# Two decoder layers on one core: the first block's attention weights turned by VectorE in squares of 32 that go round by DRAM, in place of TensorE transposes

## The chip, the cores and the metric

One core of one Trainium2 chip. The time is device microseconds of one execution; three runs of the kernel before are given. "Block" below means a block of 128 tokens: the sequence has 256, so there are two, 0 and 1. "Layer" means one of the two decoder layers.

## The reference

Each of the two layers takes x (256 tokens by 1024 channels, f32) through a half-step SwiGLU, a normalisation, three token mixers that run on the same stream, an output projection with another normalisation, and a second SwiGLU with a third. Two of the mixers are softmax attention, and the change touches only these:

```python
def memory_cross_attention(q, mem_n, w_mem_kv):
    k, v = jnp.split(mem_n @ w_mem_kv, 2, axis=-1)          # 256 memory rows, 4 heads of 128
    s = jnp.einsum('bshd,bmhd->bhsm', q, k).astype(jnp.float32) * (XA_DH ** -0.5)
    p = jax.nn.softmax(s, axis=-1)
    o = jnp.einsum('bhsm,bmhd->bshd', p.astype(v.dtype), v)

def sliding_window_attention(q, k, v, sinks):                # 8 query heads, 2 key heads of 64, window 128
    s = jnp.where(mask, einsum('bnqhgd,bnkhd->bnhgqk', qb, kb) * dh ** -0.5, NEG_INF)
    m = jnp.maximum(s.max(-1, keepdims=True), sink)
    p = jnp.exp(s - m)
    p = p / (p.sum(-1, keepdims=True) + jnp.exp(sink - m))
    o = jnp.einsum('bnhgqk,bnkhd->bnqhgd', p.astype(v.dtype), vb)
```

The third mixer is a gated delta rule with a triangular solve of 64 by 64 chunks. It is not touched, but shares the engines.

## The kernel before

All weights come as one stream of units, 128 by 1024 f32 (512 KB), in the order of use. `unit` loads one into a tile `raw` (four buffers) from the SP queue, and ScalarE and VectorE `split` it into a rounded part `whi` and a rest `wlo` (five buffers each, line 125). A product of two such split operands is three matmuls (`mm3`, line 134). TensorE therefore does 12 matmuls of 512 columns for one unit in most stages, and the other engines prepare the next units meanwhile.

A scheduler orders each engine's instructions; inside `mixers` TensorE's own are pinned to the order in which the program is written. Every engine runs its list in order: an instruction that waits holds up all that stand behind it on the same engine or queue. The DMAs that `nc.sync` starts stand in SP's list among the weight loads, those of `nc.gpsimd` in POOL's list among its arithmetic.

`weave(work, steps)` writes one stage of dense matmuls and puts small pieces of attention or delta rule between its steps. The stages of the mixers that matter here, in order, are `halves(xt, use_sq)` (four steps), `gates(0)` (eight), `branch(0, oX)` (four), `gates(1)` (eight).

- Memory attention: `x_scores(tb)` leaves the softmax of block tb in `prs[tb]`, 128 queries on the partitions by 4 heads by 256 memory rows. `x_turn(tb)` brings the memory rows to the partitions: 8 TensorE transposes of 128 by 128 through the identity (line 137) into PSUM, then one copy by ScalarE and one by VectorE into `pt` (line 711). `x_values(tb)` multiplies with the values (`at<-pt,u`).
- Sliding attention: `w_scores(tb, hh)` for two halves hh of the heads, `w_turn(tb, hh)` with the same kind of transposes and copies (line 766), `w_values(tb)` (`at<-pt,swv`). For block 0 there is one block of keys, so 4 transposes per half.
- The inverse of the delta rule: `inverses` makes, on POOL, masked copies `l` (line 798), sends a small tile to DRAM (`dr`, line 791), reads it back spread over the partitions (`w<-dr`, line 795) and runs 15 steps of elimination (lines 807 and 808), ending in `Y32` (line 809). `begin_inverse` then lets VectorE transpose it (line 902); the matmuls of `double` follow right after `w_values(0)`.

The SwiGLU stages already turn their own tiles by the way that the change uses: VectorE transposes each 32 by 32 square (line 356), four DMAs write the squares to a DRAM tile `tr` from POOL (line 362), and one DMA reads them back in the turned order (line 363).

## Time and profile before

| | |
|---|---|
| three runs | 1274.08 us median (1273.45 to 1274.12) |
| span of the profiled execution, first to last instruction | 1272.1 us |
| its own time from start to end | not given; the median of the runs is 2.0 us above its span |
| granted TensorE clock, mean | 0.998 |
| TensorE: busy time of the span | 1260.6 us, 99% |
| VectorE, ScalarE, POOL busy | 864.1, 661.4, 207.2 us |
| DMA | 261.40 MB, mean 205 GB/s |

The page lists busy time by engine, then the chain of work that ended last and the costliest groups. Because matmuls are pipelined, a group's "mean ns of one" is the time one instruction is in flight; what it costs in a row of its kind is read from the starts of neighbours in the timeline. A timeline row gives start, duration, engine, line, operation, output and inputs, the count of merged instructions, and in brackets the idle time before it with what ended it.

### The profile page before, as it was taken

How to read it: one execution, taken by the hardware profiler on the slowest of the kernel's cores; microseconds unless marked ns; L12 is line 12 of the kernel's file. 1: busy time of each engine (PE TensorE's matmuls, PEld its weight loads, DVE VectorE, ACT ScalarE, POOL GpSimd, SP SyncE). 2: the span in 40 equal slices, each digit the busy share in tenths (PEclk: the TensorE clock that was granted, in tenths of full speed). 3: DMA queues.
4: the chain of work that ended last, by engine and by line, in shares of the span. 5: the costliest groups of instructions: out<-in, count | busy, mean ns of one | idle time of the engine just before them, and what ended most of it. 6: DMA issues, size and time to landing. Idle time of an engine off the chain costs nothing.

```text
span 1272.1 us, 18768 instructions
## 1 busy us (share of the span) xinstructions
PE 1260.6 (99%) x6948; PEld 1073.3 (84%) x6948; DVE 864.1 (68%) x1274; ACT 661.4 (52%) x982; POOL 207.2 (16%) x365
## 2 busy tenths in 40 slices
PE   9999999999999999999999999999999999999997
PEld 6888889999778888888888888899987788888886
DVE  6678576886647776665766665759867387766565
ACT  6456444655664544454454554456556554454441
POOL 1232000002311102221012220000023101122100
PEclk9999999999999999999999999999999999999999
DMA  8988765655534748877668877566463356577762
GB/s 294 317 271 289 248 208 159 211 171 129 172 117 144 241 141 259 241 241 220 217 210 244 256 252 219 177 185 213 150 167 134 100 189 225 174 246 244 241 220 82
DMA packets 77643, 261.40 MB, mean 205 GB/s; under 512 B 11920, under 2 KB 13328, under 8 KB 77552
## 3 DMA queue, kind: packets, MB, share of 16 engines
q1 hardware_dynamic: 66320, 232.40, 56.0%
q0 software_dynamic: 11088, 27.68, 8.1%
q8 instruction: 54, 0.88, 0.3%
q14 instruction: 37, 0.30, 0.1%
q10 hardware_dynamic: 144, 0.13, 0.0%
HBM read 246.40 MB, written 13.76 MB: 205 GB/s over the span
## 4 chain that ended last, share of the span: by engine, by line
PE 89%; DMA 3%; POOL 3%; DVE 2%; issue 2%; ACT 0%; SPq 0%; DVEq 0%; POOLq 0%; ACTq 0%
PE acc L134 80%; PE at L134 3%; PE sm L134 2%; DMA w<-dr 2%; PE sm L137 2%; DVE wlo L125 1%; DMA raw<-in_wst_dram 1%; POOL t L808 1%; POOL t L807 1%; PE acc L332 1%; PE acc L333 1%; POOL l L798 1%; PE acc L335 1%; DMA dr<-t 1%; ACT whi L125 0%
## 5 line engine op out<-in xcount | busy, mean ns | idle before, releaser
L125 DVE TENSOR_TENSOR wlo<-raw,whi 128x1024 fp32r<-128x1024 f32 (+2 forms) x405 | 487.0, 1210 | 279.7 <-ACT whi L125 277.5
L125 ACT CAST whi<-raw 128x1024 fp32r<-128x1024 f32 (+2 forms) x405 | 413.7, 1029 | 400.6 <-PE acc L134 316.2
L134 PE MATMUL acc<-whi,hT 128*128 128x512 f32 (+1 forms) x1824 | 562.2, 386 | 0.5 <-ACT whi L125 0.5
L134 PEld LDWEIGHTS acc<-whi,hT 128*128 128x128 f32 x1824 | 340.0, 188 | 69.8 <-ACT whi L125 2.3
L134 PE MATMUL acc<-wlo,hT 128*128 128x512 f32 (+1 forms) x912 | 350.2, 384 | 0.0
L134 PE MATMUL acc<-whi,u 128*128 128x512 f32 x812 | 259.5, 392 | 0.0
L134 PEld LDWEIGHTS acc<-wlo,hT 128*128 128x128 f32 x912 | 171.3, 188 | 33.1 <-DVE wlo L125 1.0
L134 PEld LDWEIGHTS acc<-whi,u 128*128 128x128 f32 x812 | 152.3, 188 | 32.1 <-DVE u L125 0.5
L134 PE MATMUL acc<-wlo,u 128*128 128x512 f32 x406 | 158.2, 390 | 0.0
L362 POOL DMA_DIRECT2D tr<-t x176 | 96.3, 554 | 311.6 <-DVE t L356 303.5
L134 PE MATMUL acc<-hT,whi 128*128 128x256 f32 x672 | 122.2, 284 | 0.0
L134 PEld LDWEIGHTS acc<-hT,whi 128*128 128x128 f32 x672 | 104.6, 192 | 0.0
L134 PE MATMUL acc<-hT,wlo 128*128 128x256 f32 x336 | 95.0, 283 | 0.0
L134 PEld LDWEIGHTS acc<-wlo,u 128*128 128x128 f32 x406 | 76.3, 188 | 15.4
L134 PEld LDWEIGHTS acc<-hT,wlo 128*128 128x128 f32 x336 | 64.3, 191 | 0.0
L363 POOL DMA_DIRECT2D pt<-tr x44 | 25.0, 569 | 192.5 <-DMA tr<-t 138.4
L353 ACT ACTIVATE t<-acc 128x256 f32<-128x256 f32 x88 | 33.5, 381 | 36.9 <-PE acc L134 36.9
L134 PE MATMUL acc<-u,u 128*128 128x512 f32 x186 | 46.4, 394 | 0.0
L354 DVE TENSOR_TENSOR t<-t,acc 128x256 f32<-128x256 f32 x88 | 36.6, 417 | 8.1 <-ACT t L353 4.1
L1000 POOL TENSOR_TENSOR u<-u,gt 128x512 f32<-128x512 f32 x16 | 20.7, 1294 | 125.0 <-DVE gt L998 125.0
L134 PEld LDWEIGHTS acc<-u,u 128*128 128x128 f32 x186 | 34.6, 188 | 7.5
L125 DVE TENSOR_TENSOR u<-pt,u 128x512 fp32r<-128x512 f32 x44 | 28.9, 657 | 9.4 <-ACT u L125 9.4
(236 smaller groups left out, 1165.0 us busy)
## 6 DMA issues: line engine op xcount, KB each, us to landing
raw<-in_wst_dram SPq DMA_DIRECT2D x409, 512.0 KB, 4.4
tr<-t POOLq DMA_DIRECT2D x176, 64.0 KB, 3.8
pt<-tr POOLq DMA_DIRECT2D x44, 256.0 KB, 5.0
raw<-in_wst_dram SPq DMA_DIRECT2D x16, 324.0 KB, 3.0
gB<-in_lnp_dram SPq DMA_DIRECT2D x6, 512.0 KB, 5.8
bB<-in_lnp_dram SPq DMA_DIRECT2D x6, 512.0 KB, 6.2
w<-dr POOLq DMA_DIRECT2D x4, 512.0 KB, 12.0
t<-in_xT_dram SPq DMA_DIRECT2D x4, 256.0 KB, 5.2
```

What stands on the lines that cost most here:

```text
L125: return nc.scalar.copy(hi, src).ins, nc.vector.tensor_tensor(lo, src, hi.bitcast(F32), op=ALU.subtract).ins
L134: return pe(nc.tensor.matmul(*a, **k))
L137: return pe(nc.tensor.transpose(*a))
L332: nc.tensor.matmul(ps, hT[0][:, k, ts], hi[:, c], start=k == 0, stop=False)
L333: nc.tensor.matmul(ps, hT[0][:, k, ts], lo[:, c], start=False, stop=False)
L335: nc.tensor.matmul(ps, hT[1][:, k, ts], hi[:, c], start=False, stop=k == KD - 1)
L353: act = nc.scalar.activation(t[:, :, tb, :], g, AF.Silu).ins
L354: ins = nc.vector.tensor_tensor(t[:, :, tb, :], t[:, :, tb, :], u, op=ALU.mult).ins
L362: nc.gpsimd.dma_start(d[:, :, q].rearrange("b c x -> c b x"), z[32 * q:32 * q + 32].rearrange("c (b x) -> c b x", b=4))
L363: back = nc.gpsimd.dma_start(y, d.rearrange("b c q x -> (b c) (q x)")).ins
L798: nc.gpsimd.tensor_tensor(L32[q, c], AK[c][q, :, 0, q], cs[q, C_LV:C_LV + 32].unsqueeze(1).to_broadcast([32, 4, 32]), op=ALU.mult)
L1000: nc.gpsimd.tensor_tensor(mg[tb][:, js], mg[tb][:, js], gt[tb][:, js], op=ALU.add)
```

## The change

For block 0 the TensorE transposes and their copies go. A new `square` lets VectorE transpose the 32 by 32 squares of a 128 by 512 tile, writes the result to a DRAM tile by four DMAs and reads it back by one, 256 KB each way. Memory attention does this twice per layer in a new `x_leave` (POOL's queue, DRAM tile `tx`), called in step 3 of `halves(xt, use_sq)`; the call of `x_turn(0)` goes. Sliding attention does it once for each half inside `w_turn(0, hh)` (SP's queue, DRAM tile `tw`). The matmuls of `x_values(0)` and `w_values(0)` read the new layout, and the split behind `w_values(0)` becomes two splits of half the size. Block 1 stays as it is. In one run of the kernel all this happens twice, once per layer.

```diff
+        def square(src, order, queue, dst, tag):
+
+            z = T(p2, [P, 512], "t2", bufs=4)
+            nc.vector.transpose(z, src)
+            d = T(pd, [4, 32, 4, P], tag)
+            for a in range(4):
+                queue.dma_start(d[:, :, a].rearrange("m x c -> x m c"), z[32 * a:32 * a + 32].rearrange("x (m c) -> x m c", m=4))
+            order.append(lambda: queue.dma_start(dst, d.rearrange("m x a c -> (m x) (a c)")))
+
+        def x_leave():
+            pT = prs[2] = T(p2, [P, 2, 4, 4, 32], "pt")
+            backs = []
+            for kb in range(2):
+                square(prs[0][:, :, kb * P:(kb + 1) * P].rearrange("p h (m x) -> p m h x", m=4), backs, nc.gpsimd, pT[:, kb].rearrange("p a h x -> p (a h x)"), "tx")
+            for f in backs:
+                f()
+
...
-                    matmul(ps[:, h, :], mv_[:, kb, h * P:(h + 1) * P], prs[2 + tb][:, kb, h, :], start=kb == 0, stop=kb == 1)
+                    matmul(ps[:, h, :], mv_[:, kb, h * P:(h + 1) * P], prs[2 + tb][:, kb, h, :] if tb else prs[2][:, kb, :, h, :], start=kb == 0, stop=kb == 1)
...
         def w_turn(tb, hh):
             if hh == 0:
                 wpT[tb] = [T(p2, [P, 2, 4, P], "pt") for _ in range(tb + 1)]
+            if tb == 0:
+                backs = []
+                square(wpr[0, hh][:, :, 0:P].rearrange("p j (m x) -> p m j x", m=4), backs, nc.sync, wpT[0][0][:, hh].rearrange("p a x -> p (a x)"), "tw")
+                backs[0]()
+                return
...
-                    matmul(pso[hs, :], swv[:, kb, hs], wpT[tb][kb][:, kv].rearrange("p h q -> p (h q)"), start=kb == 0, stop=kb == tb)
-            split(oS[0][:, :, ts], oS[1][:, :, ts], pso.rearrange("p (h k) -> p h k", h=4))
+                    r = wpT[tb][kb][:, kv].rearrange("p h q -> p (h q)") if tb else wpT[0][0].rearrange("p y a (i v x) -> p (y a) i v x", i=2, v=2)[:, :, :, kv]
+                    matmul(pso[hs, :] if tb else pso[hs, :].rearrange("p (y i x) -> p y i x", y=8, i=2), swv[:, kb, hs], r, start=kb == 0, stop=kb == tb)
+            if tb:
+                split(oS[0][:, :, ts], oS[1][:, :, ts], pso.rearrange("p (h k) -> p h k", h=4))
+            else:
+                for y in range(2):
+                    split(*(t[:, 2 * y:2 * y + 2, ts].rearrange("p i (a x) -> p i a x", a=4) for t in oS), pso[:, y * S:y * S + S].rearrange("p (a i x) -> p i a x", a=4, i=2))
...
-            3: [lambda: spread(1)],
+            3: [lambda: spread(1), x_leave],
...
-            3: [lambda: x_turn(0)],
```

Where the scheduler puts the new instructions is read from the built programs. In the changed kernel's numbering, 711 is the write and 712 the read back of `square`, 708 its transpose, and the lines that follow them in `mixers` have moved by 27 (798 is 825, 902 is 929).

On POOL, from the two products that open the delta rule (line 678) to the inverse's DMA into `dr`, before:

```order
L678 TENSOR_TENSOR w_462_2591<-cs,g_2586 128x512
L798 TENSOR_TENSOR l_469_2600<-u_463_2592,cs 32x128 x4
L798 TENSOR_TENSOR l_469_2600<-u_464_2593,cs 32x128 x4
L803 COPY t_535_3053<-cs 128x128
L791 DMA dr_3041<-t_531_3034 128x128
```

The same place now (`tx` are the two DRAM tiles of memory attention, `pt` the turned weights that `x_values(0)` reads):

```order
L678 TENSOR_TENSOR w_462_2591<-cs,g_2586 128x512
L711 DMA tx_2925<-t_513_2923 32x4x128 x4
L711 DMA tx_2932<-t_515_2930 32x4x128 x4
L712 DMA pt_2922<-tx_2925 128x512
L825 TENSOR_TENSOR l_469_2600<-u_463_2592,cs 32x128 x4
L825 TENSOR_TENSOR l_469_2600<-u_464_2593,cs 32x128 x4
L712 DMA pt_2922<-tx_2932 128x512
L830 COPY t_540_3070<-cs 128x128
L818 DMA dr_3058<-t_536_3051 128x128
```

Ten DMAs stand ahead of the inverse's `dr`, and the second read back stands behind all eight masked copies `l`.

On VectorE, from the last sum of the sliding softmax of block 0 to the weight splits of `gates(1)`, before:

```order
L754 TENSOR_TENSOR sums_3308<-sums_3308,sk_3309 128x4
L755 RECIPROCAL sums_3308<-sums_3308 128x4
L902 STREAM_TRANSPOSE w_470_2601<-w_470_2601 128x256
L125 TENSOR_TENSOR wlo_3517<-raw_3515,whi_3516 128x1024
L125 TENSOR_TENSOR wlo_3564<-raw_3562,whi_3563 128x1024
```

The same place now (`pp_3302` is the softmax of the second half of the heads, `t_602` its turned squares):

```order
L771 TENSOR_TENSOR sums_3312<-sums_3312,sk_3313 128x4
L772 RECIPROCAL sums_3312<-sums_3312 128x4
L929 STREAM_TRANSPOSE w_470_2601<-w_470_2601 128x256
L708 STREAM_TRANSPOSE t_602_3406<-pp_3302 128x512
L125 TENSOR_TENSOR wlo_3527<-raw_3525,whi_3526 128x1024
L125 TENSOR_TENSOR wlo_3574<-raw_3572,whi_3573 128x1024
```

The second half's transpose stands behind line 929, which waits for POOL's inverse to end; the first half's (`t_599`) stands four rows ahead of line 929.

On SP's queue, among the weight loads of `gates(1)` and of what follows it, before:

```order
L115 DMA raw_3640<-in_wst_dram 128x1024
L115 DMA raw_3694<-in_wst_dram 128x1024
L115 DMA raw_3746<-in_wst_dram 128x1024
L115 DMA raw_3795<-in_wst_dram 128x1024
L115 DMA raw_3827<-in_wst_dram 128x1024
L115 DMA raw_3833<-in_wst_dram 128x1024
```

The same loads now (`tw` are the DRAM tiles of the two halves, `pt` the turned weights that `w_values(0)` reads; `raw_3650` is the load called `raw_3640` before):

```order
L115 DMA raw_3650<-in_wst_dram 128x1024
L711 DMA tw_3386<-t_599_3384 32x4x128 x4
L711 DMA tw_3408<-t_602_3406 32x4x128 x2
L712 DMA pt_3383<-tw_3386 128x512
L711 DMA tw_3408<-t_602_3406 32x4x128
L115 DMA raw_3704<-in_wst_dram 128x1024
L115 DMA raw_3756<-in_wst_dram 128x1024
L711 DMA tw_3408<-t_602_3406 32x4x128
L115 DMA raw_3805<-in_wst_dram 128x1024
L115 DMA raw_3837<-in_wst_dram 128x1024
L712 DMA pt_3383<-tw_3408 128x512
L115 DMA raw_3843<-in_wst_dram 128x1024
```

The second half's last write and its read back have moved in behind weight loads that wait for buffers. The second layer has the same orders in all three places.

## The prediction

> **What bounds the kernel now.** I read the page's busy times first, then its chain of work, then TensorE's waits, then the timeline of the mixers of the first layer.

> ```profile
> PE 1260.6 (99%) x6948; PEld 1073.3 (84%) x6948; DVE 864.1 (68%) x1274; ACT 661.4 (52%) x982; POOL 207.2 (16%) x365
> ...
> PE 89%; DMA 3%; POOL 3%; DVE 2%; issue 2%; ACT 0%; SPq 0%; DVEq 0%; POOLq 0%; ACTq 0%
> ```

> TensorE is busy for 99% of the span and carries 89% of the chain, so its work and its waits are the time. The view of waits shows how little it waits in the mixers; this is the only row there that concerns attention:

> ```profile
> PE at L134 <- DVE pp L741: 0.8, 2, 0.6
> ```

> Two waits, one in each layer, 0.8 us together and 0.6 the longest. The chain in order of time (start, duration, what) says what this wait hangs on:

> ```profile
> 306.68 3.32 DMA dr<-t
> ...
> 336.46 0.75 POOL w L809
> 337.61 0.51 DVE wlo L125
> ...
> 342.20 0.61 DVE pp L741
> 342.86 1.08 PE at L134 x4
> ```

> The inverse's trip through DRAM and its POOL work end at 337.2, VectorE's weight splits stood behind it, then its line 741, and `w_values(0)` starts 0.6 us late at 342.86. So at that place the inverse has no slack: what delays POOL's `dr` delays TensorE.

> **What is saved.** The group of the attention transposes, and TensorE's timeline in the first layer: a product of the delta rule, the 8 transposes of `x_turn(0)`, `x_values(0)`, the first `w_turn(0, .)`, `w_values(0)` and the inverse's matmuls.

> ```profile
> L137 PE MATMUL at<-cs,pp 128*128 128x128 f32 x80 | 10.9, 275 | 0.0
> ```

> ```profile
> 298.39 0.38 PE L134 MATMUL sm<-u 128*128 128x128 f32 x2
> ...
> 305.42 0.39 PE L134 MATMUL acc<-whi,hT 128*128 128x512 f32 x1
> 305.65 1.03 PE L137 MATMUL at<-cs,pp 128*128 128x128 f32 x8
> 306.44 0.48 PE L134 MATMUL acc<-whi,hT 128*128 128x512 f32 x1
> 306.76 0.39 PE L134 MATMUL acc<-wlo,hT 128*128 128x512 f32 x1
> ...
> 309.28 1.95 PE L134 MATMUL at<-pt,u 128*128 128x128 f32 x16
> 310.98 0.48 PE L134 MATMUL acc<-whi,hT 128*128 128x512 f32 x1
> ...
> 331.55 0.60 PE L137 MATMUL at<-cs,pp 128*128 128x128 f32 x4
> 331.90 0.47 PE L134 MATMUL acc<-whi,u 128*128 128x512 f32 x1
> 332.21 0.39 PE L134 MATMUL acc<-wlo,u 128*128 128x512 f32 x1
> ...
> 342.86 1.08 PE L134 MATMUL at<-pt,swv 128*64 128x512 f32 x4 [0.61 <-DVE pp L741]
> 343.86 1.51 PE L134 MATMUL sm<-w,l 32*32 32x32 f32 x64
> ```

> From 305.65 to 306.44 the 8 transposes take 0.79 us, and the matmul behind them starts its successor after 0.32 instead of 0.23 us: 0.88 us. Each half of `w_turn` takes 331.90 - 331.55 = 0.35, plus 0.08 in the same way: 0.44, and the two 0.88. Together 1.76 us per layer, 3.5 us in all. ScalarE loses three copies and VectorE one per layer, 0.6 to 0.7 us each beside dense matmuls: they count nothing.

> **What VectorE gets.** Four transposes per layer, which the SwiGLU's own show:

> ```profile
> L356 DVE STREAM_TRANSPOSE t<-t 128x512 f32<-128x512 f32 x44 | 31.3, 711 | 1.3
> ```

> 0.71 us each. The first two stand behind the softmax of block 0:

> ```profile
> 293.45 0.90 ACT L701 ACTIVATE pp<-pp,sums 128x256 f32<-128x256 f32 x2
> ```

> ```profile
> 293.91 1.22 DVE L125 TENSOR_TENSOR wlo<-raw,whi 128x1024 fp32r<-128x1024 f32 x1
> 295.05 1.26 DVE L675 SCALAR_TENSOR_TENSOR u<-w,cS,sm 128x256 f32<-128x256 f32 x3
> ...
> 337.24 0.45 DVE L902 STREAM_TRANSPOSE w<-w 128x256 f32<-128x256 f32 x1 [4.52 <-POOL w L809]
> 337.61 4.59 DVE L125 TENSOR_TENSOR wlo<-raw,whi 128x1024 fp32r<-128x1024 f32 x4
> ```

> The softmax ends at 293.45 + 0.90 = 294.35, VectorE's split at 295.1, so the transposes run to 295.8 and 296.5. The three products at 295.05 slip by 1.4 us, to 297.7; TensorE reuses their banks at 298.39, so nothing waits. The two halves of the split behind `w_values(0)` lie beside dense matmuls: nothing.

> **First wait: `x_values(0)`.** POOL's list has the eight writes, one read back, the masked copies `l`, the other read back, then the inverse's `dr`. POOL's timeline, with one set of four writes from a SwiGLU stage:

> ```profile
> 97.48 2.18 POOL L362 DMA_DIRECT2D tr<-t  x4 [3.55 <-DVE t L356]
> ...
> 296.39 2.51 POOL L798 TENSOR_TENSOR l<-u,cs 32x128 f32<-32x128 f32 x4 [14.84 <-DVE u L675]
> 302.96 3.42 POOL L798 TENSOR_TENSOR l<-u,cs 32x128 f32<-32x128 f32 x4 [4.06 <-DVE u L675]
> 306.44 0.29 POOL L803 COPY t<-cs 128x128 f32<-128x128 f32 x1
> 306.68 0.60 POOL L791 DMA_DIRECT2D dr<-t  x1
> ...
> 336.46 0.74 POOL L809 TENSOR_TENSOR w<-t,cs 128x256 f32<-128x256 f32 x1
> ```

> The next two rows are issue to landing of the SwiGLU's writes (64 KB) and read backs (256 KB), the same sizes as here:

> ```profile
> DMA to landing us min/median/max: 2.0/3.8/6.0
> ...
> DMA to landing us min/median/max: 3.1/5.0/6.9
> ```

> First four writes 295.8 to 298.0, the others to 300.2. The last of the first four starts at 297.5 and lands 3.8 later, 301.3. The read back takes 0.57 to issue (the SwiGLU's line 363 has the same shape): 301.9. Then both sets of `l`, 2.51 + 3.42 = 5.9 us: 307.8. Only then goes the second read back, and lands 5.0 later at 312.8. TensorE, 0.88 us earlier than before, stands at `x_values(0)` at 308.4: it waits **4.4 us**. With the shortest landings (2.0, where the eight writes end later, and 3.1) it is 1.4, with the longest (6.0, 6.9) 8.5. I take the medians: same sizes, same queue. Behind POOL's waits stand `l` and the inverse's `dr`, which the next part follows.

> **Second wait: `w_values(0)`.** `dr` goes at 307.8 + 0.57 + 0.29 (line 803) = 308.7 instead of 306.68, so the inverse ends 2.0 later, 339.2, and line 902 at 339.6. VectorE's order now has the second half's transpose behind line 902: 340.3. The four weight splits, 4.59 in all, end at 341.5, 342.6, 343.8 and 344.9. On SP's queue the half's fourth write stands behind two weight loads, which wait for the first two of these splits to free their buffers: it goes at 342.6 and lands 3.8 later, 346.4. The first half's read back, ahead of it, is long done. The second's follows, and `w_values(0)` needs both. For its landing I take SP's own loads:

> ```profile
> raw<-in_wst_dram SPq DMA_DIRECT2D x409, 512.0 KB, 4.4
> ```

> 4.4 us (they are twice as large, but the read back has two of them ahead): 350.8. TensorE is there at 342.25 (342.86 less its wait of 0.61) + 3.5 (first wait's end against 309.28) - 0.88 = 344.9: **5.9 us**, and the old waits are gone (0.8 in both layers). With 2.0 and 3.1 it is about 3, with 6.0 and 6.9 about 10.6. The loads on SP that are held up cost nothing more, as TensorE stands meanwhile and four split units lie ready; were that cover gone, each unit would be late by what the queue waits, 1 to 4 us.

> **After the waits.** The only long idle time of TensorE in this trace is at the start:

> ```profile
> 1.52 3.75 PE L1080 MATMUL sm<-pp 128*128 128x512 f32 x4 [1.52 <-DVE pp L1077]
> 5.04 0.74 PE L134 MATMUL acc<-whi,hT 128*128 128x512 f32 x2
> ```

> ```profile
> core 0: 1272.1 us, clock 0.998
> ```

> Four rows of f32 matmuls of 512 columns (the trace counts such a matmul twice) take 5.04 - 1.52 = 3.5 us, 0.88 each. In mid-run, 16 of 128 columns take 310.98 - 309.28 = 1.70, which is 0.43 for 512 columns. So TensorE starts at half its rate for some 3.9 us, and the run's mean granted clock leaves room for that: 0.002 x 1272 = 2.5 us. If it does so after 5.9 us of waiting, the four matmuls of `w_values(0)` (343.86 - 342.86) take 1.0 more, and I allow 0.3 for what follows, since the 64 small ones may be bound otherwise: 1.3 us, between 0 and 2.0. After 4.4 us I take none; the upper end is 1.7, the whole of `x_values(0)`.

> [...]

> **Sum.** Per layer 4.4 + 5.9 + 1.3 - 1.76 = 9.8 us. The second layer has the same orders, so I take twice that less the old waits, 19.7 - 0.8 = 18.9 us. The span of 1272.1 becomes 1291.0; the median of the runs lies 2.0 above the span, so 1293.0 us.

> [...]

> **The rivals.**
> - *Everything lands in time.* Then the transposes and the old waits go and nothing comes: 1274.1 - 3.5 - 0.8 = 1269.8, the other side. For it: `x_leave` is called two stages before its use. It needs the second read back issued by 308.4 - 5.0 = 303.4, where POOL still has its second set of `l` to do, and the second sliding half down by 344.9, 4.6 us after its transpose, with two landings between. Both would have to give way: 0.04.
> - *Only the sliding wait bites.* If the read back lands near the shortest 3.1 us and POOL's copies run faster without VectorE beside them, `x_values(0)` waits little: per layer 5.9 + 1.3 - 1.76 = 5.4, less 0.8 in all, the time 1284.2. The DMA engines' share of 0.40 in the window from 300 to 310 us (the column before the GB/s) speaks for it, the POOL order against: 0.17.

> ```profile
> 300.00:310.00 10.00, 10.00 (x54) 8.48 (x54) 7.85 (x14) 7.13 (x17) 4.02 (x6) 1.00 0.40 116
> ```

> - *Slow rate after both waits, and long landings.* `x_values(0)` at half rate adds 1.7 and the slow stretch of the second wait up to 0.7 more: 1293.0 + 4.8 = 1297.8; with landings 1 us over the median, two to a wait, 8 more, some 1306. The waits are the longest idle times of the run, the rows for it are the start's alone: 0.18.

> The change itself is done as described; the transposes really leave TensorE's list.

> **How the numbers follow.** My forecast, both waits at about the medians, has 0.61, between 1286 and 1300. Beyond it lie the sliding wait alone below and the long landings above, so 1282 to 1306 leaves about 2 in 10 out. A difference under 0.2% (2.5 us) could not be told from none. Faster by more than that is the first rival, 0.04; within it, one wait gone and the other at its shortest, 0.03; slower 0.93.

> **What would show it.** In the trace of the changed kernel: 32 fewer transposes in the group `at<-cs,pp` (48 of 80 left); TensorE idle before the first `at<-pt,u` of a layer and before the first `at<-pt,swv`, released by the DMAs `pt<-tx` and `pt<-tw`; `dr` issued some 2 us later against the POOL copies; SP's fourth `tw` write after two weight loads. The prediction is wrong if those two idle times are short, if weights come late behind SP's queue, or if TensorE stays slow for long after them.

## The result, and the profile after

The changed kernel takes 1304.03 us (median of 4 runs, 1300.28 to 1305.07); the kernel before, timed beside it, 1274.1 (4 runs, 1273.45 to 1274.55). The ratio is 1.0226, 95% interval 1.0214 to 1.0238: 29.9 us slower. The forecast was 1293.0, in a range from 1282 to 1306. The direction and the places were right; the size was not, and nearly all of this part is about where the other 11 us come from. The profiled execution took 1303.62 us with a span of 1301.8.

The busy times of the changed kernel:

```profile
PE 1268.5 (97%) x6916; PEld 1078.0 (83%) x6916; DVE 868.4 (67%) x1282; ACT 657.9 (51%) x978; POOL 218.9 (17%) x385
```

TensorE does 32 matmul rows less (6916 for 6948) and is nevertheless busy 7.9 us longer (1268.5 for 1260.6): some of its work went slower. The rest of the 29.7 us by which the span grew is idle time, and the view of TensorE's waits names it (total, times, longest):

```profile
PE at L134 <- DMA pt<-tw: 11.4, 1, 11.4
PE at L134 <- issue: 6.3, 1, 6.3
PE at L134 <- DMA pt<-tx: 4.9, 2, 2.7
```

`pt<-tw` is the read back of the sliding squares, `pt<-tx` that of the memory squares. The second row is the same place in the second layer, `w_values(0)`, where the view names no releaser; it is the read back too, which was issued at 995.19 and landed 3.2 us later, at 998.4, just ahead of the start at 998.51. So `w_values(0)` waits 11.4 and 6.3 us, `x_values(0)` 2.2 and 2.7. The group of attention transposes has shrunk as announced, from 80 rows to 48:

```profile
L137 PE MATMUL at<-cs,pp 128*128 128x128 f32 x48 | 6.4, 277 | 0.0
```

TensorE's timeline around the two places in the first layer, and `x_values(0)` and `w_values(0)` of the second:

```profile
309.80 0.38 PE L134 MATMUL at<-pt,u 128*128 128x128 f32 x2
312.37 1.83 PE L134 MATMUL at<-pt,u 128*128 128x128 f32 x14 [2.19 <-DMA pt<-tx]
...
343.90 0.39 PE L134 MATMUL acc<-whi,hT 128*128 128x512 f32 x1
355.72 1.97 PE L134 MATMUL at<-pt,swv 128*64 128x512 f32 x4 [11.43 <-DMA pt<-tw]
357.62 2.31 PE L134 MATMUL sm<-w,l 32*32 32x32 f32 x64
359.87 0.80 PE L134 MATMUL acc<-whi,hT 128*128 128x512 f32 x1
...
365.15 0.86 PE L134 MATMUL at<-swk,u 128*128 128x512 f32 x2
...
958.64 2.53 PE L134 MATMUL at<-pt,u 128*128 128x128 f32 x14 [2.70 <-DMA pt<-tx]
...
998.51 1.98 PE L134 MATMUL at<-pt,swv 128*64 128x512 f32 x4 [6.32 <-issue]
```

`x_values(0)` starts on the half that has come first, its first two rows, and then waits for the other. Behind the long wait everything is slow: the four rows of `w_values(0)` take 1.90 us (357.62 - 355.72; before 1.00), the 64 small ones 2.25 (before 1.44), and the dense matmuls from 359.87 to 365.15 take 5.3 (before 2.9). The windows around it say why. Columns: start and end, length, the engines' busy times, then the granted clock, the DMA share and GB/s:

```profile
348.00:349.00 1.00, 0.00 (x0) 0.00 (x0) 0.67 (x1) 0.00 (x0) 0.00 (x0) 0.80 1.03 331
349.00:365.00 16.00, 9.28 (x80) 6.57 (x81) 2.82 (x8) 6.20 (x18) 0.00 (x0) 0.50 0.33 116
365.00:366.00 1.00, 1.00 (x4) 0.76 (x4) 0.00 (x0) 0.61 (x1) 0.00 (x0) 0.67 0.00 0
```

The granted clock falls to a half some 4.3 us into the wait and comes back at 365.7, 10 us after TensorE has work again: 17 us of half clock (0.4 + 16 + 0.7), of which about 10 hit work. From 355.72 to 365.15, 9.4 us, TensorE does what took it 5.3 before (342.86 to 348.19): 4.1 us lost to the clock. The same reckoning gives 3.9 behind `w_values(0)` of the second layer (9.2 for 5.3), and about 1.7 behind its `x_values(0)`, where the clock is at a half for 3.4 us: its 14 rows take 2.53 us where those of the first layer take 1.83, and the rest falls on the dense matmuls behind them.

Why the squares come so late is on three other engines. POOL in the first layer, where the second read back stands behind both sets of `l`:

```profile
297.47 4.37 POOL L711 DMA_DIRECT2D tx<-t  x8 [14.50 <-DVE t L708]
301.84 0.57 POOL L712 DMA_DIRECT2D pt<-tx  x1
302.43 5.93 POOL L825 TENSOR_TENSOR l<-u,cs 32x128 f32<-32x128 f32 x8
308.30 0.60 POOL L712 DMA_DIRECT2D pt<-tx  x1
```

VectorE at the inverse's end, with the second sliding transpose behind it, and then SP's queue:

```profile
340.67 0.45 DVE L929 STREAM_TRANSPOSE w<-w 128x256 f32<-128x256 f32 x1 [4.95 <-POOL w L836]
341.04 0.67 DVE L708 STREAM_TRANSPOSE t<-pp 128x512 f32<-128x512 f32 x1
```

```profile
342.89 0.34 SPq L712 DMA_DIRECT2D pt<-tw  x1
343.28 0.42 SPq L711 DMA_DIRECT2D tw<-t  x1
343.75 0.90 SPq L115 DMA_DIRECT2D raw<-in_wst_dram  x2
344.69 0.43 SPq L711 DMA_DIRECT2D tw<-t  x1
...
350.63 0.33 SPq L712 DMA_DIRECT2D pt<-tw  x1
```

The third write goes at 343.28, two weight loads of 512 KB follow, the fourth write goes at 344.69, and SP's read back stands until that write has landed, 5.9 us later at 350.6; the read back itself takes 5.0 to land. In the second layer the same two take 5.3 and 3.2. The landing times of the tile `tw` say the same; a write with two loads ahead of it, 5.9 us, is some three times as late as the median of 1.8:

```profile
DMA to landing us min/median/max: 1.7/1.8/5.9
```

### The profile page after: what moved, and what is told of

Read it like the earlier page. It is cut to its first block, busy times and chain, and to the rows that moved or that the text cites. A ratio compares the mean times of both kernels' runs of the same rounds, so it can differ in the third digit from the quotient of the medians.

```text
span 1301.8 us, 18786 instructions
## 1 busy us (share of the span) xinstructions
PE 1268.5 (97%) x6916; PEld 1078.0 (83%) x6916; DVE 868.4 (67%) x1282; ACT 657.9 (51%) x978; POOL 218.9 (17%) x385
## 4 chain that ended last, share of the span: by engine, by line
PE 88%; DMA 5%; POOL 3%; DVE 2%; issue 1%; ACT 0%; SPq 0%; DVEq 0%; POOLq 0%; ACTq 0%
PE acc L134 78%; PE at L134 3%; PE sm L134 2%; PE sm L137 2%; DMA w<-dr 2%; DMA raw<-in_wst_dram 1%; POOL t L834 1%; DVE wlo L125 1%; PE acc L332 1%; PE acc L333 1%; PE acc L335 1%; POOL t L835 1%; DMA dr<-t 1%; POOL l L825 1%; DMA tx<-t 0%
## 5 line engine op out<-in xcount | busy, mean ns | idle before, releaser
L125 DVE TENSOR_TENSOR wlo<-raw,whi 128x1024 fp32r<-128x1024 f32 (+2 forms) x405 | 486.6, 1209 | 289.7 <-ACT whi L125 287.7
L125 ACT CAST whi<-raw 128x1024 fp32r<-128x1024 f32 (+2 forms) x405 | 413.7, 1029 | 429.8 <-PE acc L134 339.0
L134 PE MATMUL acc<-whi,hT 128*128 128x512 f32 (+1 forms) x1824 | 567.0, 389 | 0.6 <-ACT whi L125 0.6
L134 PEld LDWEIGHTS acc<-whi,hT 128*128 128x128 f32 x1824 | 343.3, 190 | 71.3 <-ACT whi L125 2.5
L134 PE MATMUL acc<-wlo,hT 128*128 128x512 f32 (+1 forms) x912 | 352.8, 387 | 0.2 <-DVE wlo L125 0.2
L134 PE MATMUL acc<-whi,u 128*128 128x512 f32 x812 | 258.4, 391 | 0.0
L134 PEld LDWEIGHTS acc<-wlo,hT 128*128 128x128 f32 x912 | 173.0, 190 | 33.7 <-DVE wlo L125 1.0
L134 PEld LDWEIGHTS acc<-whi,u 128*128 128x128 f32 x812 | 152.3, 188 | 32.2 <-DVE u L125 0.5
L134 PE MATMUL acc<-wlo,u 128*128 128x512 f32 x406 | 158.2, 390 | 0.0
L362 POOL DMA_DIRECT2D tr<-t x176 | 96.2, 553 | 308.1 <-DVE t L356 301.5
L134 PE MATMUL acc<-hT,whi 128*128 128x256 f32 x672 | 122.3, 284 | 0.0
L134 PEld LDWEIGHTS acc<-hT,whi 128*128 128x128 f32 x672 | 104.6, 192 | 0.0
L134 PE MATMUL acc<-hT,wlo 128*128 128x256 f32 x336 | 95.0, 283 | 0.0
L134 PEld LDWEIGHTS acc<-wlo,u 128*128 128x128 f32 x406 | 76.3, 188 | 15.5
L134 PEld LDWEIGHTS acc<-hT,wlo 128*128 128x128 f32 x336 | 64.3, 192 | 0.0
L134 PE MATMUL acc<-u,u 128*128 128x512 f32 x186 | 46.4, 394 | 0.0
L1027 POOL TENSOR_TENSOR u<-u,gt 128x512 f32<-128x512 f32 x16 | 20.7, 1293 | 124.5 <-DVE gt L1025 124.5
L134 PEld LDWEIGHTS acc<-u,u 128*128 128x128 f32 x186 | 34.6, 188 | 7.5
L553 DVE SCALAR_TENSOR_TENSOR t<-acc,cw,t 128x255 f32<-128x255 f32 (+2 forms) x72 | 34.5, 479 | 1.0
## 6 DMA issues: line engine op xcount, KB each, us to landing
raw<-in_wst_dram SPq DMA_DIRECT2D x409, 512.0 KB, 4.4
gB<-in_lnp_dram SPq DMA_DIRECT2D x6, 512.0 KB, 6.2
bB<-in_lnp_dram SPq DMA_DIRECT2D x6, 512.0 KB, 6.4
w<-dr POOLq DMA_DIRECT2D x4, 512.0 KB, 10.1
```

The source lines that it names most:

```text
L125: return nc.scalar.copy(hi, src).ins, nc.vector.tensor_tensor(lo, src, hi.bitcast(F32), op=ALU.subtract).ins
L134: return pe(nc.tensor.matmul(*a, **k))
L362: nc.gpsimd.dma_start(d[:, :, q].rearrange("b c x -> c b x"), z[32 * q:32 * q + 32].rearrange("c (b x) -> c b x", b=4))
L553: nc.vector.scalar_tensor_tensor(yc[:, j, d:], b[:, j, :S - d], w[:, t:t + 1], yc[:, j, d:], op0=ALU.mult, op1=ALU.add)
L1027: nc.gpsimd.tensor_tensor(mg[tb][:, js], mg[tb][:, js], gt[tb][:, js], op=ALU.add)
```

## The experiments

Twelve kernels, each timed against the kernel before on the same chip (whose medians there are 1274.4 to 1275.1; beside the changed kernel it was 1274.1, so differences of a microsecond between kernels timed apart mean nothing). Line numbers move by a few between them: 708 or 710 is the squares' transpose, 929 or 934 the inverse's, 711 and 712 (713, 714) the write and the read back, 760 the masking of `w_scores` (758 in the kernel after, 741 in the one before).

**One part alone.** First the memory squares with the sliding transposes on TensorE, then the reverse.

```diff
-            if tb == 0:
-                backs = []
-                square(wpr[0, hh][:, :, 0:P].rearrange("p j (m x) -> p m j x", m=4), backs, nc.sync, ...)
-                backs[0]()
-                return
...
```

> Only the memory weights of block 0 go round by DRAM; the sliding ones are turned on TensorE as before. Theory one, the inverse has no slack: x_values(0) waits 2.2 and 2.7 us as in the changed kernel and runs slow once (1.5), the eight transposes save 0.88 per layer, and the inverse, which ends 3.4 us later than before (340.6 against 337.2), is met by w_values(0), whose old wait of 0.6 grows to about 2.7: 4.4 us per layer, 1274.1 + 8.9 = 1283. Rival, the later inverse is covered: only the waits at x_values(0) count, 1274.1 + 4.9 + 1.5 - 1.8 = 1278.7, and w_values(0) waits 0.6 or less.

Measured: 1279.57 us (5 runs), ratio 1.0031 [1.0018, 1.0044]; 4.5 us slower. The rival's time was right.

```profile
PE at L134 <- DMA pt<-tx: 4.9, 2, 2.5
...
PE at L134 <- DVE pp L758: 0.4, 2, 0.2
```

```profile
308.75 0.55 POOL L808 DMA_DIRECT2D dr<-t  x1
...
322.18 1.48 POOL L824 TENSOR_TENSOR t<-w,t 128x120 f32<-128x120 f32 x1 [7.73 <-DMA w<-dr]
```

`dr` goes 2.1 us later than before (306.68), but its read back lands sooner, so that POOL's recurrence starts at 322.18, earlier than before (322.82). The delay of `dr` was not handed on, the inverse ended at 337.7 (before 337.2), and `w_values(0)` waits 0.4 in both layers together. So the rival's reason was not put to the test: there was no late inverse to be covered. Half clock stood behind both waits at `x_values(0)`, 3.4 us each, where the rival counted one.

```diff
-            3: [lambda: spread(1), x_leave],
+            3: [lambda: spread(1)],
...
+            3: [lambda: x_turn(0)],
```

> Only the sliding weights of block 0 go round by DRAM; the memory ones are turned on TensorE as before. Theory one, the sliding round trip has its own cost whatever the memory part does: waits of about 11 and 6 us at w_values(0), some 4 us of half clock behind each, 0.88 saved per layer and the old waits gone: 1274.1 + 17.7 + 8 - 1.8 - 0.8 = 1297. Rival, the sliding wait is long because the memory part makes the inverse 3.4 us late: with the inverse at 337.2 again the second transpose, its writes and read back come 3.4 us earlier, the waits are about 8 and 3, the second one is too short for the clock to fall, and the time is about 1287.

Measured: 1295.82 us, ratio 1.016 [1.0145, 1.0175]; 20.7 us slower. The wait view:

```profile
PE at L134 <- DMA pt<-tw: 8.9, 1, 8.9
PE at L134 <- DVE sums L771: 8.1, 1, 8.1
```

The second row is `w_values(0)` of the second layer. It names VectorE's line 771, but that line writes nothing that `w_values(0)` reads; the read back, issued at 987.62, landed about 3.1 us later, and TensorE started at 990.89. That is 17.0 us of waiting without any memory square in the program. The first theory holds in the sum, though not layer by layer (it had 11 and 6): the sliding part has its own cost. That a wait of about 3 us is too short for the clock to fall, as the rival took it, no run shows: behind the 2.70 us at `x_values(0)` of the changed kernel it was at a half for 3.4 us. The two parts alone add up to 25.2 us, the whole is 29.9; what is left over was not followed further.

**What sets the sliding wait.** Two orders stood against each other: VectorE's, which puts the second transpose behind the inverse's, and SP's, which puts two weight loads ahead of the fourth write. The first edit lets the inverse's transpose follow the squares' (`wpr["turned"]`):

```diff
-            with tc.issue_after(wpr["end"]):
+            with tc.issue_after(wpr["turned"]):
                 nc.vector.transpose(W[:, 512:768], W[:, 768:1024])
```

> The changed kernel, with one order on VectorE turned round: the second sliding transpose goes ahead of the inverse's transpose (line 929) and runs at 337.1 instead of 341.04, when its weights are ready. SP's order is the same. Theory one, SP's queue sets the wait: the fourth write still stands behind two weight loads that wait for the weight splits, which come only 0.7 us earlier, so w_values(0) still waits about 10.5 us (after: 11.4) and the time is 1302 to 1304. Rival, the order on VectorE sets it: everything behind the transpose comes 4 us earlier, the waits are 7.4 and 2.3 instead of 11.4 and 6.3, and the time is 1296 or, if the clock then stays up in the second layer, 1292.

Measured: 1298.71 us, ratio 1.0181 [1.0166, 1.0197]: 5.3 us under the changed kernel, between the two theories. The transpose ran at 336.15, 4.9 us earlier, yet `w_values(0)` still waited 9.8 and 6.5 us. SP's queue shows the reason:

```profile
338.91 0.42 SPq L711 DMA_DIRECT2D tw<-t  x1
341.64 1.49 SPq L115 DMA_DIRECT2D raw<-in_wst_dram  x2
343.17 0.43 SPq L711 DMA_DIRECT2D tw<-t  x1
```

The third write is out at 338.91, and SP then stands until 341.64 for the weight splits that its next two loads need. The fourth write, whose data have long been ready, waits behind them. The second edit puts the four loads in question behind the read back (`back`, of the half `hh` = 1):

```diff
+                if hh:
+                    first[:] = [None] * 6 + [back] * 4
...
+                with tc.issue_after(first[0]) if first and first[0] else nullcontext():
                     nc.sync.dma_start(raw[:, c], src[:, c])
```

> The changed kernel, with one order on SP turned round: the four weight loads that stood between the fourth sliding write and its read back go behind both. VectorE's order of the second transpose is the same (it ends at 341.7). Theory one, SP's queue sets the wait: the fourth write goes about 343, lands 1.8 later as the others do, the read back lands about 3.5 behind that, 348.5: w_values(0) waits about 4 us instead of 11.4, in the second layer about 2 instead of 6.3; the clock falls less or not at all: 1304 - 7.4 - 4 - 4 to 8 = 1285 to 1289. Rival, the transport itself is slow at this place (landings of 5.9 and 5.0 whatever stands ahead): the writes land at 349, the read back at 354, the wait stays about 10 us and the time about 1302.

Measured: 1288.59 us (1282.92 to 1291.14), ratio 1.0098 [1.0068, 1.0128]: 15.4 us less, with VectorE's order untouched.

```profile
341.66 0.90 SPq L713 DMA_DIRECT2D tw<-t  x2
344.65 0.34 SPq L714 DMA_DIRECT2D pt<-tw  x1
```

```profile
347.18 1.08 PE L136 MATMUL at<-pt,swv 128*64 128x512 f32 x4 [4.03 <-DMA pt<-tw]
348.19 2.22 PE L136 MATMUL sm<-w,l 32*32 32x32 f32 x64
```

The third and fourth write go together, the read back 3.0 us after the third, and it lands 2.5 later: the wait is 4.0 us, and 2.0 in the second layer, where the view names VectorE's line 766 but the read back landed at 984.6 and TensorE started at 984.75. SP's queue is the main cause; the transport as such is quick, 3.0 and 2.5 us. With two 512 KB loads ahead of it the fourth write took 5.9 us to land in the changed kernel; in this run no write of `tw` took more than 3.0.

Both orders together:

> The changed kernel with both orders turned round at the sliding part: the second transpose ahead of the inverse's on VectorE, and the four weight loads behind the read back on SP. Theory, the two orders are the whole of the sliding wait: the transpose ends at 336.9, the four writes are down by 341, the read back by 344, about when TensorE comes (343.3 in the run with VectorE's order alone): w_values(0) waits 1 us or less in each layer, no half clock there, and what is left over the kernel before is the memory part (+4.5 in its own run) less 1.8 of sliding transposes and 0.8 of old waits: 1276 to 1278. Rival, a third cause (the landing of writes and read back themselves): 2 to 4 us of wait stay in each layer, 1281 to 1286.

Measured: 1282.18 us, ratio 1.0051 [1.0033, 1.0069]. The squares now come in time in the first layer (1.2 us of wait for `pt<-tw` in the second), but not 1277: a third cause, and not the landing.

```profile
PE at L136 <- DVE pp L760: 3.3, 3, 1.7
```

The longest of the three stands at `w_values(0)` of the first layer, which needs a PSUM bank that VectorE's line 760 of `w_scores(1, 0)` has to read out first. This is the wait that the kernel before has at its line 741 (0.6 there); it was not gone, it lay hidden under the longer one. The other two, 0.8 each, stand at `w_scores(1, 1)`, where the kernel before has none; both runs that have SP's order so far show them. The memory part, with 5.5 us of waits at `x_values(0)`, is as it was.

**POOL's order.** The copies `l` go behind the second read back, `dr` and the read backs of `dr` (`fetched` is the last of them).

```diff
+            with tc.issue_after(fetched):
                 for c in range(2):
                     for q in qd:
                         nc.gpsimd.tensor_tensor(L32[q, c], ...)
```

> The changed kernel with one order on POOL turned round: the eight masked copies l (5.9 us) go behind the second memory read back, the inverse's write dr and its two read backs. Theory, POOL's order sets the first wait: the read back goes when the last memory write has landed, about 305, and lands at 309, before TensorE comes at 310.2: x_values(0) waits 0 to 0.5 instead of 2.2 and 2.7, dr goes about 4 us earlier, the inverse ends earlier by as much, and the sliding wait shrinks to the 8 to 9 us that it has with the sliding part alone: 1292 to 1296. Rival, the landings set it: the read back waits for the last write until 305 or later and needs 5 us more, x_values(0) still waits 1.5 or more; or the eight copies, now late, hold the first stage of the inverse's doubling: 1299 to 1303.

Measured: 1297.52 us, ratio 1.0169 [1.015, 1.0187]. The wait at `x_values(0)` is gone in both layers, and the sliding one, with SP's order as it was, is all that is left:

```profile
PE at L134 <- DMA pt<-tw: 21.1, 2, 10.8
```

So POOL's order, not the landing, made the first wait. That the sliding wait did not shrink to 8 or 9 us, as the theory had it, is a miss: `dr`, no longer behind the copies, now waited 1.1 us for its own data and went at 307.78; the inverse ended 2.8 us earlier than in the changed kernel (337.8), but TensorE came to `w_values(0)` 3.3 us earlier. In the second layer the wait grew from 6.3 to 10.3; why was not followed.

All three orders:

> The changed kernel with all three orders turned round (POOL's, VectorE's, SP's). Theory, every wait of the change is one of order: TensorE keeps the 1.76 us of transposes per layer and the old waits go, with at most 1 us of new wait in each layer: 1274 - 3.5 - 0.8 + 0 to 2 = 1270 to 1272, faster than the kernel before by 0.2 to 0.3%. Rival, the round trips cost something that no order hides (later weights behind SP's read back, the weight splits later on VectorE, the longer start of the memory part): 1274 to 1278, no gain.

Measured: 1279.53 us (12 runs, 1278.53 to 1284.55), ratio 1.0037 [1.0025, 1.0048]. No gain, so the theory failed. In the profiled execution, the longest of the twelve (granted clock 0.991, the others 0.993 to 0.997), 6.7 us of waits stand at line 760: 2.45 and 2.65 at `w_values(0)`, with half clock behind both, and 0.8 at `w_scores(1, 1)` in each layer. VectorE in the first layer:

```profile
337.38 0.45 DVE L934 STREAM_TRANSPOSE w<-w 128x256 f32<-128x256 f32 x1 [3.20 <-POOL w L841]
337.74 4.59 DVE L127 TENSOR_TENSOR wlo<-raw,whi 128x1024 fp32r<-128x1024 f32 x4
342.25 1.28 DVE L760 SCALAR_TENSOR_TENSOR pp<-at,cs 128x512 f32<-128x512 f32 x2
```

VectorE stands 3.2 us for POOL's inverse, then does four weight splits, and only then the masking that frees the bank; TensorE, earlier by the transposes it no longer does, waits 2.45 us for it. The fourth order puts the inverse's transpose behind the masking (`wpr["masked"]` is its instruction):

```diff
-            with tc.issue_after(wpr["turned"]):
+            with tc.issue_after(wpr["masked"]):
                 nc.vector.transpose(W[:, 512:768], W[:, 768:1024])
...
-            3: [lambda: w_turn(0, 1), begin_inverse],
-            4: [lambda: w_scores(1, 0)]})
+            3: [lambda: w_turn(0, 1)],
+            4: [lambda: w_scores(1, 0), begin_inverse]})
```

> The kernel with all three orders, and a fourth turned round on VectorE: the inverse's transpose goes behind the four weight splits and the two maskings of w_scores(1,0) (line 760), instead of ahead of them. Theory, what was left there (6.7 us in four waits, 2.45 in the first layer) is that chain: w_values(0) needs a PSUM bank that line 760 frees, which stands behind four splits, which stand behind a transpose that waits for POOL; with the order turned the bank is free at 339.9, TensorE comes at 340.5, and the waits and the half clock behind them go: 1279.5 - 6.7 - 1 to 4 = 1269 to 1272, under the kernel before. Rival, the inverse's first matmuls behind w_values(0) now wait for the later transpose, or something else comes last there: 1274 to 1279.

Measured: 1272.60 us (12 runs, 1271.60 to 1274.52; before 1274.36), ratio 0.9986 [0.9977, 0.9996]. This is the only version below the kernel before, by 1.8 us, and 31 below the change as it was made. It still waits 3.1 us at `w_values(0)`, and the second of these waits brings a stretch of half clock:

```profile
PE at L136 <- DVE w L934: 3.1, 2, 1.8
```

The view names line 934, the inverse's transpose, but the trace says that it is the read back:

```profile
339.23 0.34 SPq L714 DMA_DIRECT2D pt<-tw  x1
```

It landed 2.6 us after its issue, at 341.8; line 934 had ended at 341.4, and TensorE started at 341.96. In the second layer it landed 2.6 after 968.07, and TensorE started at 970.80. So what is left of the wait is the round trip itself, 8.7 us from the second transpose's start at 333.16 to its landing.

The control is the kernel before with the two orders that it can take as well:

> The kernel before, all transposes on TensorE, with the two orders that it can take too: the masked copies l behind dr on POOL, and the inverse's transpose behind the two maskings on VectorE. Theory, these are worth only the old waits of 0.8 us: 1273 to 1274, the same as before within what can be told, and a gain of the kernel with all four orders comes from the transposes. Rival, the orders are worth more than the waits show, 1270 to 1272, and the turning by squares itself gives nothing.

Measured: 1274.12 us, ratio 0.9996 [0.9987, 1.0006]. The orders alone give nothing that can be told from none; the kernel with the squares and all four orders is 1.5 us under this control. And the memory squares alone with these two orders:

> Only the memory weights go round by DRAM, with the same two orders (POOL's copies l, and the inverse's transpose behind the maskings). Theory, its wait at x_values(0) is gone and with it all that this part cost: its eight transposes per layer save 0.88 us, the old waits 0.8 in all: 1274.6 - 1.8 - 0.8 = 1272. Rival, DMAs and VectorE's two transposes cost what the transposes save: 1274 to 1276.

Measured: 1274.64 us, ratio 1.0000 [0.9990, 1.0010]. The 4.5 us that this part cost are gone, and no gain shows: it keeps 1.5 us of waits at its line 758 that the kernel before has as 0.8. So the 1.5 us come with the sliding squares or with both kinds together; which was not separated.

**What the slow clock costs.** Matmuls whose result nobody reads fill most of the sliding wait.

```diff
+        def fill():
+            ps = sm()
+            for _ in range((6, 12)[l == 0]):
+                matmul(ps, ident, cs[:, 0:512], start=True, stop=True)
...
-            1: [lambda: w_values(0), double],
+            1: [fill, lambda: w_values(0), double],
```

> The changed kernel with idle matmuls put ahead of w_values(0) on TensorE, 12 in the first layer and 6 in the second, of 128 rows and 512 columns of f32 (about 0.86 us each at the full rate), whose result nobody reads. They fill 10.3 of the 11.4 us of wait and 5.2 of the 6.3. Theory, the half clock behind the wait comes from TensorE's idle time: the four matmuls of w_values(0) take 1.0 us again instead of 1.9, the dense ones behind them 2.9 instead of 5.3, and the time falls by 4.2 + 3.8 = 8 us to 1296, although the wait as such is not a microsecond shorter. Rival, the slow rows have another cause (the DMA's late landing, the operands' layout in squares): they stay slow, and the time is 1304, or more by what the filling overshoots.

Measured: 1296.44 us (1293.39 to 1300.25), ratio 1.0162 [1.0139, 1.0184]: 7.6 us under the changed kernel, as the theory had it.

```profile
355.06 1.08 PE L134 MATMUL at<-pt,swv 128*64 128x512 f32 x4
356.06 1.51 PE L134 MATMUL sm<-w,l 32*32 32x32 f32 x64
```

`w_values(0)` starts within 0.7 us of where it does in the changed kernel, but its four rows take 1.00 again, and the 64 small ones 1.51 instead of 2.31 (the time in flight, as the rows have it). No half clock stands there in either layer. At `x_values(0)` this execution happened to lose more than the changed kernel (7.4 us of waits for 4.9), so the rows at `w_values(0)` say more than the total. Since only TensorE's idle time was taken away, the half clock behind the wait comes from that idle time: a quarter of the whole loss.

**Using the squares later.** `w_values(0)` and the first stage of the doubling one step further, on top of all four orders:

```diff
-            1: [lambda: w_values(0), double],
-            2: [lambda: w_scores(1, 1)],
-            3: [double],
+            2: [lambda: w_values(0), double],
+            3: [lambda: w_scores(1, 1), double],
```

> The kernel with all four orders, and w_values(0) with the first stage of the doubling one step of gates(1) later (behind the second weight unit, w_scores(1,1) one step later too): TensorE has some 3 us of dense matmuls more before it needs the squares. Theory, the 3.1 us of wait that the kernel with four orders still has at w_values(0) are hidden: 1272.6 - 3.1 = 1269 to 1270, what the removed transposes are worth (1274.4 - 3.5 - 0.8). Rival, the later stage of the doubling or the later w_scores(1,1) meets its own wait further on (the inverse's chain with one step less between two stages): 1272 to 1276.

Measured: 1279.15 us, ratio 1.0031 [1.0020, 1.0042]. The rival was right:

```profile
PE sm L136 <- ACT w L893: 3.7, 2, 1.8
PE at L136 <- DVE pp L760: 1.9, 2, 1.1
```

The waits at `w_values(0)` are gone, and two kinds stand behind them: a later stage of the doubling waits for ScalarE, whose copies (line 893) are now among the softmax of `w_scores(1, 1)`, with 3.4 us of half clock behind each of these waits; and `w_scores(1, 1)` waits for its bank.

## Why the prediction was right, and where its sum was not

*What bounds it, and where the change bites.* Right. TensorE's waits are the time, and both forecast places showed them, released by the DMAs that were named.

*The saving.* Right: 48 of 80 transposes are left. For `x_turn(0)` the kernel with all four orders gives a clean reading, since nothing waits there:

```profile
298.19 0.38 PE L136 MATMUL sm<-u 128*128 128x128 f32 x2
...
308.17 1.95 PE L136 MATMUL at<-pt,u 128*128 128x128 f32 x16
```

From the delta rule's product to `x_values(0)` it takes 9.98 us, before 309.28 - 298.39 = 10.89: 0.91 saved, forecast 0.88.

*VectorE's transposes and the three products that slip.* Right, no wait appears there.

*First wait, 4.4 us forecast, 2.2 and 2.7 measured.* The order on POOL was read rightly, and the second read back goes at 308.30 (forecast 307.8). Two sizes were off: it lands 4.0 us later, not 5.0 (the trace's median for it is 4.0), and TensorE is there at 310.2, not 308.4, of which 1.4 us are there before anything that the change touches has run (a row that stands at 258.27 in the kernel before stands at 259.69 in the changed one). Both make the wait shorter. The copies ahead of it took 5.93 us, forecast 5.9, so they were not the faster ones of the second rival; in the kernel before such copies took from 0.45 to 1.33 us each, the longest, at 305.1, while VectorE did a weight split.

*Second wait, 5.9 us forecast, 11.4 and 6.3 measured.* The chain was right link by link: the inverse, line 929, the second transpose, the fourth write behind two loads. The fourth write went at 344.69 (forecast 342.6), since the inverse ended 1.4 us later than forecast and the write waited somewhat more for the loads. The term that failed is its landing: 3.8 us were taken from POOL's writes, which have no 512 KB loads ahead of them in their queue, where the prediction had just said that this one has two; it took 5.9. The read back took 5.0 for 4.4. The run with SP's order shows both numbers without the loads: 2.5 and 2.5. The bounds in the prediction, about 3 and 10.6, leave TensorE and the inverse where the medians put them. Carried through, the shortest landings give 4.7 and the longest 8.7, since a shorter first wait brings TensorE forward by more than the inverse.

*The old waits, taken as gone (0.8).* Wrong in kind: they were covered by the new wait and came back, larger, as soon as that was shortened (at `w_values(0)` 1.7 us with two orders and 5.1 with three; before 0.8).

*Slow TensorE, 1.3 us per layer forecast, 4.1 and 3.9 measured, and about 1.7 after the first wait of the second layer, for which none was taken.* This is the largest error, and one that the prediction had named itself as a sign of being wrong, that TensorE stays slow for long after the waits. It took the length of the slow stretch, 3.9 us, from the start of the kernel before. The rows there do run at half their later pace (0.88 us each; 0.43 in the fill run), but the granted clock of the windows is full there, and what the mean of 0.998 lacks stands at the end, from 1268.5 us on, where TensorE has no more work:

```profile
0.00:3.00 3.00, 1.48 (x2) 0.83 (x3) 0.58 (x3) 2.25 (x3) 0.30 (x5) 1.00 0.35 103
3.00:6.00 3.00, 3.00 (x6) 0.88 (x5) 1.39 (x2) 1.87 (x4) 0.00 (x0) 1.00 0.93 283
```

So no row of the kernel before showed what a wait costs in clock, and why its start is slow is not shown. After the long wait the stretch was 17 us, 10 of them over work. The fill experiment gives 7.6 us for the two long waits, where the trace gives 4.1 + 3.9.

*`dr` delayed, so the inverse is late, so TensorE is late.* In the changed kernel `dr` went 3.5 us later than before, 1.4 of them from the start, and the inverse ended 3.4 later (340.6 for 337.2): the delay was handed on. In the run with the memory part alone it was not: from `dr` to POOL's recurrence it took 13.4 us there, 16.1 before and 15.9 in the changed kernel. Why `w<-dr` landed sooner in that run is not shown.

*Sum.* Forecast 18.9 us, measured 29.9 by the medians. The first waits are 3.9 us smaller (4.9 for 8.8), the second 5.9 larger (17.7 for 11.8), the slow clock 7.1 larger (9.7 for 2.6), and the start of the profiled run adds 1.4: 18.9 + 10.5 = 29.4, against the 29.7 of the two spans. The time lies where the third rival put it, 1297.8 to 1306, slow clock and late landings, beyond the 1300 that the main case reached to. So the range held by a rival that had 0.18, and that one was right only in part: `x_values(0)` ran slow in one layer, not in both, and the landings of the first wait were under the medians, not over. The errors of the two waits also cancel in part, which is luck. The first rival, everything in time, took four changes of order to come near, 1272.6 where it has 1269.8.

## What to carry to other kernels

A round trip through DRAM is priced by the queue it goes through: count what stands ahead of each of its DMAs on its own queue, and of each instruction behind it on the engine, and take the landing from rows of that queue (the 64 KB writes of `tw` on SP's landed after 1.8 us at the median, and after 5.9 behind two weight loads). Where TensorE is the bound, an idle stretch on it can cost twice, once as a wait and again as slow matmuls behind it (2.7 and about 1.7 us at `x_values(0)` of the changed kernel's second layer), so a saving of 0.9 us is no reason to risk a wait of two. And a short wait that vanishes under a longer one is still there (0.6 us before, 1.7 with two orders): when the longer one is cut, it is the next to come.

## What the runs showed of the hardware that was not expected

The stretches of half clock came in steps. Counted in windows of 1 us they were 3.4 us long after the waits of 2.4 and 2.5 us in the memory part's run, 10 us after 2.45 us in the run with three orders, and 17 after 11.4 us, 7 of these within the wait. And a wait of 1.4 us in the second layer of the kernel with four orders had one behind it, though TensorE had work again by then, while the 1.8 us of its first layer had none:

```profile
972.00:973.00 1.00, 1.00 (x54) 1.00 (x53) 0.64 (x3) 0.81 (x4) 0.00 (x0) 0.87 0.85 320
973.00:976.00 3.00, 3.00 (x24) 2.45 (x20) 1.70 (x5) 3.00 (x12) 0.00 (x0) 0.50 0.93 365
976.00:977.00 1.00, 1.00 (x6) 0.83 (x5) 0.30 (x1) 0.16 (x1) 0.00 (x0) 0.92 0.57 135
```
